# A tile of h in two VectorE instructions with a column each, and one ScalarE pass

## The chip, the cores and the metric

The kernel runs on one core of a Trainium2 chip. The metric is device time in microseconds for one execution; three runs of the kernel before took 1175.74, 1176.55 and 1177.19 us, and their median, 1176.55, is the time to compare with. The engines are named as in the profile: PE is TensorE's matmuls, PEld its weight loads, DVE is VectorE, ACT is ScalarE, POOL is GpSimd, and SP is the queue that starts most transfers.

## What is computed

A decoder trunk of two layers on one sequence of 512 tokens with 1024 channels. Layer 0 mixes tokens with stick-breaking attention, layer 1 with a diagonal state-space layer; each is followed by a gated FFN with a short causal convolution. In front of every mixer and every FFN stands the same small step, and it is the one that the change touches:

```python
def rms_norm(x, g):
    y = xf * lax.rsqrt(jnp.mean(xf * xf, axis=-1, keepdims=True) + EPS)
    return (y * g.astype(jnp.float32)).astype(x.dtype)

def modulate(h, shift, scale):
    return h * (1 + scale[:, None, :]) + shift[:, None, :]
...
    h = modulate(rms_norm(x, norm_mix[i]), sh1, sc1)
```

So h is x times a factor per token (the reciprocal root), times a weight per channel (norm gain times one plus scale), plus a shift per channel. Shift and scale come from a conditioning vector through a matrix-vector product.

## The kernel before

All activations lie transposed: 8 tiles `x[k]` of 128 channels by 512 tokens. Every matrix product is made in three terms for accuracy: each operand is held as a high part (rounded to the matmul's type) and a low part (the value less its high part), and `mm3` (lines 169 to 175) issues high times high, low times high and high times low. In the traces the three have lines 171, 174 and 175. Each weight tile is split in the same way when it arrives (`load_w`, lines 147 to 167): a transfer by SP, the high part on ScalarE (line 165), the low part on VectorE (line 166).

The tiles of h are made by `norm_tile` (lines 302 to 323). For tile k it issues:

- line 308, VectorE: t = x[k] times the factor per token. The factor was broadcast to all partitions by a matmul, so that it is a tile `bc`; in a head it lies in PSUM and is made in two halves of 256 tokens (a full tile then takes two instructions), in attention a copy `rb` in SBUF is used;
- line 315, ScalarE: the high part of t times the weight column `a[:, k]` plus the shift column `b[:, k]`;
- line 317, ScalarE: the same value once more, at full precision, into a tile u;
- line 321, VectorE: the low part, u minus the high part.

The trace names t and u both "nt", the high parts "hH", the low parts "hL", and the weight columns "Amix", "Anorm_ffn" and "Anorm_mix" after the norm that they belong to.

`norm_tile` has two callers.

In attention's V projection (lines 683 to 696) it makes tiles 1 to 7 in full width, one for each turn of a loop; tile 0 is made by hand by other lines (629 to 671), which keep both ScalarE passes. In a turn, ScalarE also makes the high part of the next weight tile (line 568), and the two columns of the next tile (lines 580 and 586) out of row sums that VectorE makes (line 198, a product with accumulation over 1024 columns). VectorE also makes the low part of the weight tile (line 686). Here the instructions are pinned in the order in which the program writes them: `mid` (lines 684 to 688) is placed between the ScalarE passes and the subtraction.

In `head_mm` (lines 326 to 340), which opens the first FFN (near 262 us), the state-space layer (near 634 us) and the second FFN (near 801 us), it makes six tiles in halves, the first half of each and later the second, and then two full tiles: 14 calls. The four output tiles of the head multiply each half as soon as it is there. Within the first halves, at fixed places of TensorE's order, stand the row statistic of the second half (line 266, at tile 1) and the broadcast of its factor (line 288, at tile 3); between them lie a root on ScalarE, five tiny VectorE instructions and the scale matrix `dg` (line 283). The head runs while VectorE still adds the last output tiles of the layer before to the residual (line 355) and sums their squares (lines 244 and 245).

The order of each engine's queue is made at build time by a planner, which simulates the program with a cost for each instruction. What the program pins (`pe_pin`, `keep_in_program_order`) keeps its written order; `follow` and `issue_after` keep an instruction behind another; all the rest goes where the planner's simulation has it ready. The list `pin["head"]` keeps the ScalarE and VectorE instructions of each tile: the weight loads after a head and the preparation of the state-space layer are issued behind them (`behind_head`, lines 342 to 347).

Of the kernel before, what the change touches and what calls it, by code (L numbers as in the profile page):

```python
# [7 lines left out]
F32 = mybir.dt.float32  # L8
# [3 lines left out]
AF = mybir.ActivationFunctionType  # L12
ALU = mybir.AluOpType
# [3 lines left out]
P = 128  # L17
T = 512
# [66 lines left out]
def trunk(tc, I, out, tap=lambda *a: None):  # L85
    with ExitStack() as ctx:
        _trunk(ctx, tc, I, out, tap)


def _trunk(ctx, tc, I, out, tap):  # L90
    nc = tc.nc
    V, S, G, PE, SP = nc.vector, nc.scalar, nc.gpsimd, nc.tensor, nc.sync

    def pool(name, bufs=1, **kw):
        return ctx.enter_context(tc.tile_pool(name=name, bufs=bufs, **kw))
# [5 lines left out]
    np_ = pool("np")  # L101
# [9 lines left out]
    x = [xp.tile([P, T], F32, tag=f"x{k}", name=f"x{k}") for k in range(KD)]  # L111
# [25 lines left out]
    pin = {"head": []}  # L137
# [69 lines left out]
    def mcol(l, v, j):  # L207
        return l * 48 + v * 8 + j
# [90 lines left out]
    def half_cols(ap, cr):  # L299
        return ap.rearrange("p (j c) -> p j c", j=CH)[:, :, cr.start // CH:cr.stop // CH]  # L300

    def norm_tile(h, k, bc, a, b, cr=FULL, pinned=False, first=None, mid=None):
        n = cr.stop - cr.start
        t = np_.tile([P, T], F32, tag="nt1", bufs=2, name="nt1")[:, :n]
        u = np_.tile([P, T], F32, tag="nt2", bufs=1, name="nt2")[:, :n]
        for part in HALF if cr == FULL and isinstance(bc, dict) else (cr,):
            src = bc[part.start] if isinstance(bc, dict) else bc
            pin["nt"] = V.tensor_tensor(t[:, part.start - cr.start:part.stop - cr.start], x[k][:, part], src[:, part], ALU.mult)
        hh, hl = h[0][k][:, cr], h[1][k][:, cr]
        hf = hh.bitcast(F32)  # L310
        keep = pe_pin if pinned else lambda ins: None
        keep(pin["nt"])
        if first:
            first()
        act = S.activation(hh, t, AF.Identity, bias=b[:, k:k + 1], scale=a[:, k:k + 1])
        keep(act)
        aff = S.activation(u, t, AF.Identity, bias=b[:, k:k + 1], scale=a[:, k:k + 1])
        keep(aff)
        if mid:
            mid()  # L320
        dve = V.tensor_tensor(hl, u, hf, ALU.subtract)
        keep(dve)
        pin["head"].append([act, aff, dve])


    def head_mm(R, h, a, b, hd):
        pin["head"] = []
        todo = [(k, HALF[0]) for k in range(HEADK)] + [(k, HALF[1]) for k in range(HEADK)] + [(k, FULL) for k in range(HEADK, KD)]
        made = 0
        for n, (k, cr) in enumerate(todo):  # L330

            while made < (min(n + 3, HEADK) if cr == HALF[0] else n + 1):
                norm_tile(h, todo[made][0], R["bc"], a, b, todo[made][1])
                made += 1
            for q, (w, ps) in enumerate(hd):
                if cr == HALF[0] and (k, q) == HEADS:
                    rstd_stat(R, HALF[1], True)
                if cr == HALF[0] and (k, q) == HEADB:
                    rstd_bc(R, HALF[1], mm, True)
                mm3(ps[:, cr], wk(w, k), (h[0][k][:, cr], h[1][k][:, cr]), k == 0 and cr.start == 0, k == KD - 1)  # L340
# [201 lines left out]
    def attention(acc):  # L542
        with ExitStack() as av_, ExitStack() as ac:
# [139 lines left out]
            for k in range(1, KD):  # L683
                def mid():
                    nxt[0] = high(k + 1) if k < KD - 1 else None
                    pe_pin(V.tensor_tensor(w[1], raws[k], w[0].bitcast(F32), ALU.subtract))
                    if k < KD - 1:
                        gv(1, k + 1)

                nxt = [None]  # L690
                gv(0, k)
                norm_tile(h, k, rb, a, mod[:, 0:KD], FULL, True, None, mid)
                if k + 2 < KD:
                    raws[k + 2] = loads(k + 2)
                prods(k, w)
                w = nxt[0]
# [787 lines left out]
    b = mod[:, mcol(2, 0, 0):mcol(2, 0, 0) + KD]  # L1484
# [154 lines left out]
```

## Time and profile before

The profile shows one execution; the durations in the prediction come from it.

| | |
|---|---|
| median of three runs | 1176.55 us |
| the profiled execution's own time | 1175.82 us |
| its span, first to last instruction | 1174.0 us |
| mean granted TensorE clock | 0.995 |
| data moved | 211.01 MB, 180 GB/s on average |

The span is 1.82 us shorter than the execution's own time. The page gives each engine's busy time and instruction count (the number after the x). A line of a group has the source line, the engine, the operation, output and inputs by name, shapes, the count, then busy time and the mean ns of one, and the idle time of the engine in front of it with what ended it. A line of the timeline has start, duration, engine, source line, operation and names; a bracket shows the idle time in front of it. A matmul's duration there includes the filling of its pipeline, so that matmuls in a row overlap, and the distance from start to start is what one costs. Rows of a table of stretches have start and end, the length, the busy time of PE, PEld, DVE, ACT and POOL with counts, the clock, the share of the DMA engines and GB/s.

### The profile page before, as it was taken

What the parts mean: (1) busy time and instruction counts of PE and PEld (TensorE: products, weight loads), DVE (VectorE), ACT (ScalarE), POOL (GpSimd) and SP (SyncE); (2) the same over time, 40 slices, a digit from 0 to 9 for tenths busy, and PEclk for the clock granted to TensorE, in tenths of its full rate; (3) what the DMA queues carried; (4) which work ended last, traced back from release to release, by engine and by line L of the source; (5) the groups of instructions that cost most, each with busy time, mean ns of one, the idle gap of its engine ahead of it and who ended that gap; (6) DMA issues with size and microseconds to landing.
All of it is one profiled execution on the core that took longest, in us unless ns stands there. A gap on an engine that the chain in (4) does not pass through costs nothing.

```text
span 1174.0 us, 16592 instructions
## 1 busy us (share of the span) xinstructions
PE 1158.9 (99%) x6242; PEld 964.2 (82%) x6242; DVE 857.7 (73%) x1311; ACT 563.5 (48%) x896; POOL 270.8 (23%) x278
## 2 busy tenths in 40 slices
PE   8999999999999999999999999999999999999997
PEld 7887777699788888888889888789888888888887
DVE  6968888775998666787757599887598378744555
ACT  6756667456453244413346477647443144422443
POOL 2001110000298799979800000000000000000003
PEclk8999999999999999999999999999999999999999
DMA  8873656331267858797756598671176357432322
GB/s 320 292 264 116 192 162 195 111 123 55 78 189 268 247 167 252 198 292 253 230 151 223 149 353 293 207 255 50 49 231 217 107 153 184 133 123 73 92 69 72
DMA packets 91618, 211.01 MB, mean 180 GB/s; under 512 B 19601, under 2 KB 37905, under 8 KB 91538
## 3 DMA queue, kind: packets, MB, share of 16 engines
q1 hardware_dynamic: 78562, 191.08, 51.0%
q0 software_dynamic: 4656, 16.78, 4.5%
q10 hardware_dynamic: 8320, 2.10, 0.8%
q8 instruction: 49, 0.80, 0.3%
q14 instruction: 31, 0.25, 0.1%
HBM read 188.68 MB, written 21.24 MB: 179 GB/s over the span
## 4 chain that ended last, share of the span: by engine, by line
PE 78%; DVE 7%; issue 7%; DMA 5%; ACT 2%; POOL 1%; SPq 1%; POOLq 0%; DVEq 0%; ACTq 0%
PE up L171 13%; PE up L174 13%; PE up L175 13%; PE dn L171 6%; PE dn L174 6%; PE dn L175 6%; DMA wg<-in_w_modT_dram 3%; PE u L174 1%; PE u L171 1%; PE u L175 1%; PE wo L171 1%; PE wos L174 1%; PE wo L175 1%; PE wo L174 1%; PE wos L175 1%
## 5 line engine op out<-in xcount | busy, mean ns | idle before, releaser
L171 PE MATMUL up<-hH,up_h 128*128 128x512 f32 x640 | 249.7, 391 | 0.3 <-DVE ca L461 0.3
L175 PE MATMUL up<-hH,up_l 128*128 128x512 f32 x640 | 249.3, 390 | 0.3 <-DVE up_l L166 0.3
L174 PE MATMUL up<-hL,up_h 128*128 128x512 f32 x640 | 249.3, 390 | 0.0
L461 DVE SCALAR_TENSOR_TENSOR ca<-up,small,ca 128x511 f32<-128x511 f32 (+1 forms) x176 | 131.6, 748 | 120.7 <-ACT ca L459 117.6
L171 PE MATMUL dn<-gH,dn_h 128*128 128x512 f32 (+1 forms) x394 | 145.0, 369 | 0.0
L198 DVE SCALAR_TENSOR_TENSOR wg<-wg,cact 128x1024 f32<-128x1024 f32 x96 | 121.4, 1281 | 31.7 <-DMA wg<-in_w_modT_dram 31.6
L174 PE MATMUL dn<-gL,dn_h 128*128 128x512 f32 (+1 forms) x394 | 144.5, 367 | 0.0
L175 PE MATMUL dn<-gH,dn_l 128*128 128x512 f32 (+1 forms) x394 | 144.4, 366 | 0.0
L171 PEld LDWEIGHTS up<-hH,up_h 128*128 128x128 f32 x640 | 120.1, 188 | 26.5 <-issue 1.5
L175 PEld LDWEIGHTS up<-hH,up_l 128*128 128x128 f32 x640 | 120.1, 188 | 25.9 <-DVE up_l L166 1.1
L174 PEld LDWEIGHTS up<-hL,up_h 128*128 128x128 f32 x640 | 120.1, 188 | 24.4
L459 ACT ACTIVATE ca<-up,small 128x512 f32<-128x512 f32 x88 | 68.2, 775 | 149.5 <-PE up L175 149.5
L1511 POOL TENSOR_SCALAR xa<-x,Anorm_out 128x256 f32<-128x256 f32 x7 | 5.7, 818 | 570.3 <-DVE x L355 570.3
L165 ACT ACTIVATE up_h<-up_r 128x1024 fp32r<-128x1024 f32 x80 | 84.2, 1052 | 75.3 <-PE dn L174 58.1
L166 DVE TENSOR_TENSOR up_l<-up_r,up_h 128x1024 fp32r<-128x1024 f32 x80 | 116.3, 1454 | 5.4 <-ACT up_h L165 4.5
L355 DVE SCALAR_TENSOR_TENSOR x<-dn,mod,x 128x512 f32<-128x512 f32 (+1 forms) x55 | 37.4, 680 | 71.4 <-PE dn L175 71.4
L171 PEld LDWEIGHTS dn<-gH,dn_h 128*128 128x128 f32 x394 | 74.3, 189 | 12.9 <-issue 0.6
L174 PEld LDWEIGHTS dn<-gL,dn_h 128*128 128x128 f32 x394 | 74.3, 189 | 12.1
L175 PEld LDWEIGHTS dn<-gH,dn_l 128*128 128x128 f32 x394 | 74.3, 189 | 12.1
L165 ACT ACTIVATE dn_h<-dn_r 128x1024 fp32r<-128x1024 f32 (+1 forms) x48 | 46.7, 982 | 46.2 <-PE dn L174 38.5
L166 DVE TENSOR_TENSOR dn_l<-dn_r,dn_h 128x1024 fp32r<-128x1024 f32 (+1 forms) x48 | 61.6, 1283 | 0.8 <-ACT dn_h L165 0.5
L477 ACT ACTIVATE gH<-gm 128x512 fp32r<-128x512 f32 x44 | 27.1, 616 | 67.3 <-DVE gm L473 67.3
(349 smaller groups left out, 2311.0 us busy)
## 6 DMA issues: line engine op xcount, KB each, us to landing
up_r<-in_w_up_dram SPq DMA_DIRECT2D x80, 512.0 KB
wg<-in_w_modT_dram SPq DMA_DIRECT2D x71, 512.0 KB
dn_r<-in_w_down_dram SPq DMA_DIRECT2D x32, 512.0 KB
wg<-in_w_modT_dram POOLq DMA_DIRECT2D x25, 512.0 KB, 4.0
wgs<-in_w_modT_dram SPq DMA_DIRECT2D x16, 512.0 KB
dn_r<-in_w_down_dram SPq DMA_DIRECT2D x16, 384.0 KB
wv_r<-in_w_v_dram SPq DMA_DIRECT2D x8, 512.0 KB
wk_r<-in_w_qk_dram SPq DMA_DIRECT2D x8, 512.0 KB
```

Source lines behind the costliest of these rows:

```text
L165: order("S", lambda: S.activation(wh[:, :n], raw[:, :n], AF.Copy))
L166: pin["split"] = order("V", lambda: V.tensor_tensor(wl[:, :n], raw[:, :n], wh[:, :n].bitcast(F32), ALU.subtract))
L171: ins = PE.matmul(ps, ah, bh, start=start, stop=False)
L174: PE.matmul(ps, ah, bl, start=False, stop=False)
L175: PE.matmul(ps, al, bh, start=False, stop=stop)
L198: mul = lambda: V.scalar_tensor_tensor(w, w, 1.0, cact, ALU.mult, ALU.mult, accum_out=raw[:, col:col + 1])
L355: add = lambda: V.scalar_tensor_tensor(xs, pv, gate, xs, ALU.mult, ALU.add)
L459: follow("S", lambda: S.activation(ca, ps, AF.Identity, bias=small[:, cb:cb + 1], scale=tapw[2]))
L461: follow("V", lambda: V.scalar_tensor_tensor(ca[:, q:], ps[:, :T - q], tapw[2 - q], ca[:, q:], ALU.mult, ALU.add))
L477: follow("S", lambda: S.activation(gh, m, AF.Copy))
L1511: G.tensor_scalar(xa[k], x[k][:, cb], a[:, k:k + 1], 0.0, ALU.mult, ALU.add)
```

## The change

The product on line 308 takes the weight column along: (x times a) times the factor, one three-operand VectorE instruction. ScalarE then only adds the shift and rounds to the high part. The second ScalarE pass and its tile u are gone; the subtraction becomes (t plus shift) minus the high part, again one three-operand VectorE instruction. `pin["head"]` keeps two instructions for each tile in place of three. Tile 0 of attention, which has its own lines, isn't changed, and no transfer is.

```diff
     def norm_tile(h, k, bc, a, b, cr=FULL, pinned=False, first=None, mid=None):
         n = cr.stop - cr.start
         t = np_.tile([P, T], F32, tag="nt1", bufs=2, name="nt1")[:, :n]
-        u = np_.tile([P, T], F32, tag="nt2", bufs=1, name="nt2")[:, :n]
         for part in HALF if cr == FULL and isinstance(bc, dict) else (cr,):
             src = bc[part.start] if isinstance(bc, dict) else bc
-            pin["nt"] = V.tensor_tensor(t[:, part.start - cr.start:part.stop - cr.start], x[k][:, part], src[:, part], ALU.mult)
+            pin["nt"] = V.scalar_tensor_tensor(t[:, part.start - cr.start:part.stop - cr.start], x[k][:, part], a[:, k:k + 1], src[:, part], ALU.mult, ALU.mult)
         hh, hl = h[0][k][:, cr], h[1][k][:, cr]
-        hf = hh.bitcast(F32)
...
-        act = S.activation(hh, t, AF.Identity, bias=b[:, k:k + 1], scale=a[:, k:k + 1])
+        act = S.activation(hh, t, AF.Identity, bias=b[:, k:k + 1])
         keep(act)
-        aff = S.activation(u, t, AF.Identity, bias=b[:, k:k + 1], scale=a[:, k:k + 1])
-        keep(aff)
         if mid:
             mid()
-        dve = V.tensor_tensor(hl, u, hf, ALU.subtract)
+        dve = V.scalar_tensor_tensor(hl, t, b[:, k:k + 1], hh.bitcast(F32), ALU.add, ALU.subtract)
         keep(dve)
-        pin["head"].append([act, aff, dve])
+        pin["head"].append([act, dve])
```

## Prediction

> **What bounds the kernel now.** I read the page first, then the busy time in the four stretches where the changed helper runs, then who waits for whom, and last the timeline around each wait.
>
> ```profile
> span 1174.0 us, 16592 instructions
> ...
> PE 1158.9 (99%) x6242; PEld 964.2 (82%) x6242; DVE 857.7 (73%) x1311; ACT 563.5 (48%) x896; POOL 270.8 (23%) x278
> ```
> ```profile
> 22.00:66.00 44.00, 44.00 (x195) 36.27 (x195) 40.99 (x60) 32.28 (x56) 0.00 (x0) 1.00 0.85 276
> ...
> 255.00:300.00 45.00, 45.00 (x298) 41.09 (x297) 28.41 (x81) 25.75 (x43) 0.18 (x2) 1.00 0.16 48
> ...
> 632.00:660.00 28.00, 27.75 (x201) 26.06 (x200) 20.37 (x53) 21.78 (x39) 0.00 (x0) 1.00 0.50 175
> ...
> 800.00:835.00 35.00, 35.00 (x231) 31.83 (x230) 20.90 (x46) 23.20 (x38) 0.00 (x0) 1.00 0.18 61
> ```
>
> TensorE is busy for 1158.9 of 1174.0 us. The columns of the second answer are the stretch, its length, then PE, PEld, DVE, ACT and POOL busy, the clock, and DMA. The first stretch is the V projection of attention, which calls the helper for tiles 1 to 7. The other three are the heads of the first FFN, of the state-space layer and of the second FFN, where the helper makes h from the residual. In the first, second and fourth TensorE is never without a matmul. In the third it lacks 0.25 us. So ScalarE's load there (half to four fifths of the time) is not what ends these stretches. It can matter only where TensorE stands for a tile of h. The next answers show who stands for the operation that goes.
>
> ```profile
>   DVE hL L321: 10.7, 21
> ```
> ```profile
> PE u L174 <- DVE hL L321: 0.2, 1, 0.2
> ```
> ```profile
> PEld up L174 <- DVE hL L321: 0.6, 2, 0.3
> ```
>
> The first line is from the view of line 317, the second ScalarE pass, under those who waited for it: VectorE's low-part subtraction stood 10.7 us in 21 places. The other two are from TensorE's and the weight loads' lists of waits: of those 10.7 us only one matmul and two weight loads pass anything on. All the other idle time of VectorE is hidden behind matmuls already queued.
>
> **The change, part by part.** The helper runs 49 times: three heads with 12 half tiles (256 columns) and 2 full tiles (512), and seven full tiles in V. These are the prices of what it issues, and of the nearest operations of the forms that it will issue.
>
> ```profile
> L317 ACT ACTIVATE nt<-nt,mod,Anorm_ffn 128x256 f32<-128x256 f32 x24 | 14.3, 596 | 0.3 <-DVE hL L321 0.3
> L315 ACT ACTIVATE hH<-nt,mod,Anorm_ffn 128x256 fp32r<-128x256 f32 x24 | 14.2, 590 | 4.5 <-DVE nt L308 4.5
> ...
> L315 ACT ACTIVATE hH<-nt,mod,Amix 128x512 fp32r<-128x512 f32 x7 | 5.7, 817 | 2.2 <-DVE nt L308 2.1
> ```
> ```profile
> L459 ACT ACTIVATE ca<-up,small 128x512 f32<-128x512 f32 x88 | 68.2, 775 | 149.5 <-PE up L175 149.5
> ...
> L813 ACT ACTIVATE wT<-t,ones 128x512 f32<-128x512 f32 x16 | 10.3, 684 | 24.5 <-PE t L810 24.5
> ```
> ```profile
> L461 DVE SCALAR_TENSOR_TENSOR ca<-up,small,ca 128x511 f32<-128x511 f32 x88 | 65.8, 747 | 117.9 <-ACT ca L459 117.6
> ...
> L308 DVE TENSOR_TENSOR nt<-x,rbc 128x256 f32<-128x256 f32 x48 | 18.9, 415 | 2.1 <-PE rbc L288 2.0
> ...
> L321 DVE TENSOR_TENSOR hL<-nt,hH 128x256 fp32r<-128x256 f32 x36 | 15.3, 424 | 7.8 <-ACT nt L317 7.6
> ...
> L355 DVE SCALAR_TENSOR_TENSOR x<-wos,mod,x 128x512 f32<-128x512 f32 x5 | 6.0, 1206 | 0.0
> ...
> L1322 DVE TENSOR_TENSOR m<-pv,pR 128x512 f32<-128x512 f32 x8 | 5.5, 690 | 9.7 <-PE pv L1280 9.6
> ...
> L308 DVE TENSOR_TENSOR nt<-x,rb 128x512 f32<-128x512 f32 x7 | 4.8, 683 | 0.0
> ```
>
> Removed: 49 ScalarE passes, 36 of 256 columns at 0.596 us (21.5 us) and 13 of 512 at about the 0.817 of their twin on line 315 (10.6 us), together 32 us of ScalarE's 563.5. On the path of one tile that is one ScalarE pass less between the first product and the low part.
>
> Changed on ScalarE: the high part loses its scale column and keeps its bias column. Line 459 has both columns and takes 775 ns, line 813 has the bias column alone and takes 684 ns, both from PSUM, so I take 0.09 us off each of the 49; the bounds are no gain and 0.13 us (817 less 684, which mixes sources).
>
> Changed on VectorE: 55 products (48 of half tiles, 7 of full ones) and 49 subtractions become three-operand instructions with a column. Line 461 is that form: 747 ns against 683 for the plain product, so 0.064 us more each, 104 x 0.064 = 6.7 us of VectorE in all. The bounds are no cost and the dearest such row, line 355 on wos, whose operands are strided: 1206 less 683, 0.52 us each. I take 0.064, since line 461 has contiguous operands, as the new ones do. Lines 1322 and 308 have one PSUM source and none, and cost 690 and 683, so the 64 ns are the column's rather than PSUM's.
>
> [...]
>
> What hides the 6.7 us. In a head a half tile feeds 12 matmuls of about 0.12 us (half the slot of a 512-column one, below), 1.4 us, and VectorE's two operations for it are 0.415 + 0.424 + 2 x 0.064 = 0.97 us; VectorE was idle for 27 to 40% of the head stretches, and of its 10.7 us of standing most go. In V the cover is thinner, and shown below.
>
> What TensorE gets back. These rows show the three places where it stood for hL.
>
> ```profile
> 634.65 0.73 PE L171 MATMUL u<-hH,win_h 128*128 128x256 f32 x4
> 635.63 0.38 PE L174 MATMUL u<-hL,win_h 128*128 128x256 f32 x1 [0.24 <-DVE hL L321]
> ```
> ```profile
> 634.76 0.48 DVE L355 SCALAR_TENSOR_TENSOR x<-dn,mod,x 128x256 f32<-128x256 f32 x1 [0.46 <-PE dn L175]
> 635.16 0.41 DVE L321 TENSOR_TENSOR hL<-nt,hH 128x256 fp32r<-128x256 f32 x1
> ```
> ```profile
> 634.51 0.59 ACT L317 ACTIVATE nt<-nt,mod,Anorm_mix 128x256 f32<-128x256 f32 x1
> ```
> ```profile
> 272.49 0.39 PE L171 MATMUL up<-hH,up_h 128*128 128x512 f32 x1
> 272.87 0.39 PE L174 MATMUL up<-hL,upo_h 128*128 128x256 f32 x1
> ```
> ```profile
> 811.43 0.39 PE L171 MATMUL up<-hH,up_h 128*128 128x512 f32 x1
> 811.79 0.39 PE L174 MATMUL up<-hL,uph_h 128*128 128x256 f32 x1
> ```
>
> State-space head: four 256-column matmuls start at 634.65. Their 0.73 us covers a filled pipeline, and they leave it free for the next from about 635.13 to 635.39; the next starts at 635.63, so 0.24 to 0.50 us are lost. Line 317 ended at 635.10 and the subtraction came at 635.16, but behind a residual update on VectorE (634.76, 0.48) that waits for TensorE. With line 317 gone the subtraction is ready about when that pass used to start, 634.51, ahead of that update, if the planner puts it there; then all of the loss goes. If it stays behind, nothing goes, and the longer form adds 0.06. I take 0.4 saved, bounds -0.5 and +0.06.
>
> FFN heads: a 512-column matmul takes one slot of about 0.23 us (V's 24 per tile in 5.44 us, below). The next follow after 0.38 and 0.36 us, so 0.15 and 0.13 are lost. The subtraction now ends about 0.5 us sooner, so both go: 0.28 saved, bounds -0.28 and 0. What is late next is the last matmul in front, that is TensorE itself.
>
> The added wait. The product now reads the scale column, which ScalarE alone read before. In the heads that column is a vector written long before (first and second FFN):
>
> ```profile
> L229 DVE SCALAR_TENSOR_TENSOR Anorm_ffn<-mod,small x2: 159/161/163, 197.3 to 791.0; 128x8 f32<-128x8 f32 x2
> ```
>
> The heads' first products come at 260 and 799 us. In V it is made column by column by ScalarE, and behind a product that waits for it stand, on VectorE's queue, the weight split of the same tile, the next column's row sum, and the low part.
>
> ```profile
> 29.89 0.68 DVE L308 TENSOR_TENSOR nt<-x,rb 128x512 f32<-128x512 f32 x1
> ...
> 34.52 0.68 DVE L308 TENSOR_TENSOR nt<-x,rb 128x512 f32<-128x512 f32 x1
> ...
> 53.05 0.69 DVE L308 TENSOR_TENSOR nt<-x,rb 128x512 f32<-128x512 f32 x1
> ```
> ```profile
> 43.36 1.98 PE L171 MATMUL v<-wv_h,hH 128*128 128x512 f32 x8
> ...
> 48.80 1.98 PE L171 MATMUL v<-wv_h,hH 128*128 128x512 f32 x8
> ```
> ```profile
> 52.37 0.39 ACT L586 ACTIVATE Amix<-mod,small 128x1 f32<-128x1 f32 x1
> ```
>
> VectorE's turn is 34.52 - 29.89 = 4.63 us and has no gap; TensorE's is 48.80 - 43.36 = 5.44 us. With two dearer operations VectorE's becomes 4.63 + 0.13 = 4.76, still shorter. At the upper bound it would be 4.63 + 1.05 = 5.68, and TensorE would lose 0.24 us in each of six turns, 1.4 us. The column for the last tile is written by 52.76 and wanted at 53.05: a margin of 0.29 us, and VectorE can lose 0.68 us in a turn before TensorE notices. So V is worth 0, bounds 0 and +1.4.
>
> Nothing is moved past a DMA queue: the helper issues no transfer, and the weight loads that follow a tile keep the high and low parts as their marks.
>
> The sum: -0.4 - 0.28 + 0 = about -0.7 us, bounds -0.8 and +1.5. The profiled execution took 1175.82 us (span 1174.0 and 1.82 around it) and would take 1175.1; the median of the three runs, 1176.55, lies 0.73 above it, so I predict 1175.85 us. A measurement of this kernel can tell about 0.2%, 2.35 us, from no change, and 0.7 is 0.06%.
>
> **The rivals.** First, every chain start is paid back: each head has two half-tile chains, and if TensorE's queue were refilled a whole ScalarE pass sooner in all six, 6 x 0.596 = 3.6 us would go, 1173.0 us. For it: the passes are in series with the first low part. Against it: only three of the six have a wait at all, and TensorE's whole shortage there is known.
>
> Second, VectorE's standing is what sets the pace, and its 10.7 us come off: 1165.9 us. Against it stand the stretches with TensorE never idle. [...]
>
> Third, slower: the second half's statistic comes late. In a head the scale matrix dg of the second half passes through VectorE's queue, and its broadcast on TensorE stands at a fixed place in the order, with the rest of the head behind it.
>
> ```profile
> 267.98 0.48 DVE L283 TENSOR_SCALAR dg<-consts,ny 128x128 f32<-128x128 f32 x2
> 268.38 1.22 DVE L166 TENSOR_TENSOR up_l<-up_r,up_h 128x1024 fp32r<-128x1024 f32 x1
> ```
> ```profile
> 270.17 0.59 PE L288 MATMUL rbc<-dg,ones 128*128 128x256 f32 x2
> ```
>
> dg ends at 268.46 and the broadcast starts at 270.17: 1.7 us of cover. The weight split behind it (1.22 us) waits for a ScalarE pass, and with ScalarE lighter it can be ready before dg. A plan that puts this split and two tiles' pairs (2 x 0.97) ahead of dg delays it 3.16 us, 1.45 past the cover, 4.4 us in three heads: 1180.9 us. It decides from a delay of 1.7 us in a head, and is over 2.35 us in sum from 2.5. For it: these instructions are left to the planner. Against it: the tiles themselves finish sooner, so one split alone (1.22) fits the cover, and the pairs have mostly gone by then.
>
> That the change doesn't do what it says can't be: two instructions of each tile become one form and a third is not issued.
>
> **How the numbers follow.** Forecast, small gain or none with V's bound inside: 0.80. All chain starts: 0.06. VectorE's standing: 0.02. Late statistic, or another order of the planner that costs over 2.35 us: 0.12, since the order is made anew for the whole program, and TensorE's idle time to be won by one is only 1174.0 - 1158.9 = 15 us in all, while what can be lost has no such end. Faster by over 0.2% is 0.06 + 0.02 = 0.08, same 0.80, slower 0.12. The range goes down to 1174.2, which is past the lower bound (1175.75) less the spread of the runs (lowest 1175.74, 0.81 below the median) and ends where faster begins. It goes up to 1178.7, the upper bound of +1.5 and the spread on that side (1177.19, 0.64 above). What it leaves out is the 0.08 and the 0.12, 0.2 in all.
>
> **What would show it.** Right: line 317's group gone; the high part at about 0.50 us (256) and 0.72 (512); product and subtraction near 0.48 and 0.75; the waits of TensorE for hL gone or under 0.1; VectorE's turn in V near 4.76 us, without a gap ahead of the product, and TensorE's unchanged at 5.44; the head stretches shorter by some tenths. Wrong: TensorE idle in front of the second broadcast, a VectorE gap that ends with the scale column in V, or a difference of more than 2.35 us in a stretch where the helper doesn't run, which would be the planner's.

## The result and the profile after

The changed kernel takes 1182.80 us (median of four runs, 1181.24 to 1184.79) against 1176.14 for the kernel before (four runs, 1175.49 to 1177.19): a ratio of 1.0057, 95% interval 1.0037 to 1.0076, slower by 6.7 us. Run once more (e7 below, six runs) it took 1184.24 against 1176.14, ratio 1.0067 (1.0051 to 1.0082). The prediction, 1175.85 within 1174.2 to 1178.7, was wrong, on the wrong side.

In the changed kernel line 315 is line 314, line 321 is line 318, and whatever lies behind the helper is three lines higher up (most of the later runs have the old numbers there). First the page, then groups of instructions, with shapes kept apart.

```profile
span 1182.1 us, 16546 instructions
...
PE 1160.6 (98%) x6242; PEld 964.2 (82%) x6242; DVE 861.4 (73%) x1311; ACT 533.1 (45%) x847; POOL 275.0 (23%) x278
```
```profile
L314 ACT ACTIVATE hH<-nt,mod 128x256 fp32r<-128x256 f32 x36 | 17.1, 503 | 27.7 <-DVE nt L308 26.6 <-PE wo L175 1.0
L318 DVE SCALAR_TENSOR_TENSOR hL<-nt,mod,hH 128x256 fp32r<-128x256 f32 x36 | 16.3, 478 | 1.1 <-ACT hH L314 1.1
...
L318 DVE SCALAR_TENSOR_TENSOR hL<-nt,mod,hH 128x512 fp32r<-128x512 f32 x13 | 9.4, 746 | 0.0
L314 ACT ACTIVATE hH<-nt,mod 128x512 fp32r<-128x512 f32 x13 | 9.4, 722 | 2.6 <-DVE nt L308 2.5
...
L308 DVE SCALAR_TENSOR_TENSOR nt<-x,Amix,rb 128x512 f32<-128x512 f32 x7 | 5.2, 746 | 0.4 <-ACT Amix L583 0.4
```

The instructions cost what was forecast: 0.48 and 0.75 us on VectorE, 0.50 and 0.72 on ScalarE, and ScalarE is lighter by 30 us. VectorE's low part stands for ScalarE for 1.1 us, where it stood for 10.7. Yet the span of the profiled execution grew by 8.1 us. The next two views say where: the busy time in the three heads, over the same stretches as in the prediction, and the list of what TensorE waited for.

```profile
255.00:300.00 45.00, 43.88 (x305) 40.73 (x305) 28.65 (x75) 17.03 (x30) 0.18 (x2) 1.00 0.19 58
632.00:660.00 28.00, 26.50 (x210) 25.38 (x209) 22.06 (x57) 11.71 (x23) 0.00 (x0) 1.00 0.40 152
800.00:835.00 35.00, 33.89 (x251) 31.95 (x250) 22.93 (x56) 11.83 (x23) 0.00 (x0) 1.00 0.16 48
```
```profile
PE up L171 <- ACT hH L314: 2.2, 2, 1.1
...
PE t L807 <- DVE om L795: 1.9, 5, 0.6
PE wo L174 <- DVE oL L927: 1.6, 1, 1.6
PE pz L1351 <- ACT yn L1346: 1.6, 3, 0.6
PE pk L1137 <- POOL cl L1200: 1.2, 1, 1.2
PE u L171 <- ACT hH L314: 1.1, 1, 1.1
```

TensorE was never idle in the two FFN heads and lacked 0.25 us in the other. Now it lacks 1.12, 1.50 and 1.11 us. In each head it stands once, for 1.1 us, for a high part. Two more names come back below: pk is a product in the preparation of the state-space layer, which falls into the first FFN's stretch and reads a table cl made by GpSimd; pz is a transpose in that layer, which reads a copy yn made by ScalarE. So the kernel got slower just where the prediction said that nothing could be late.

One head in detail. The first fence is TensorE's timeline of the kernel before, the second the same place after; both begin with the statistic of the second half.

```profile
265.94 0.50 PE L266 MATMUL stat<-ones,acc 128*128 128x1 f32 x4
...
270.42 0.82 PE L171 MATMUL up<-hH,upo_h 128*128 128x256 f32 x4
271.07 0.28 PE L174 MATMUL up<-hL,upo_h 128*128 128x256 f32 x1
...
272.02 0.63 PE L171 MATMUL up<-hH,upo_h 128*128 128x256 f32 x4
```
```profile
271.01 0.50 PE L266 MATMUL stat<-ones,acc 128*128 128x1 f32 x4
...
274.81 0.28 PE L175 MATMUL up<-hH,upo_l 128*128 128x256 f32 x1
274.93 0.59 PE L288 MATMUL rbc<-dg,ones 128*128 128x256 f32 x2
276.64 0.74 PE L171 MATMUL up<-hH,upo_h 128*128 128x256 f32 x4 [1.11 <-ACT hH L314]
```

Before, the broadcast (270.17) was followed by the 12 matmuls of the last first-half tile, from 270.42 to 272.02, and under them the first tile of the second half was made. After, nothing of the first half is left behind the broadcast, so TensorE stands from the end of the broadcast until that tile comes. VectorE isn't the one that is late:

```profile
267.84 0.42 DVE L245 TENSOR_TENSOR acc<-acc,sq 128x256 f32<-128x256 f32 x1
...
272.69 0.49 DVE L283 TENSOR_SCALAR dg<-consts,ny 128x128 f32<-128x128 f32 x2
```

The sum of squares is complete at 268.26, and the statistic comes 2.75 us later. dg ends at 273.18, 1.75 us ahead of the broadcast, about the cover of 1.7 us that it had before. It is TensorE's own order that holds both back. I had called their places fixed, and they are not: a pinned instruction is only kept behind the one in front of it in the program, and the matmuls of later tiles, which aren't pinned, may pass. In the built programs, compared with each other, the second half's statistic stands 15, 4 and 15 matmuls later in the three heads, its broadcast 12, 20 and 12. There are 21 pieces in a different order in TensorE's queue, 22 in VectorE's, 11 in ScalarE's and 5 in SP's, in V, the heads and around the state-space layer.

### The profile page after: what moved, and what is told of

The parts are those of the page before. It is cut to its first block, busy times and chain, and to the rows that moved or that the text cites. A ratio compares the mean times of both kernels' runs of the same rounds, so it can differ in the third digit from the quotient of the medians.

```text
span 1182.1 us, 16546 instructions
## 1 busy us (share of the span) xinstructions
PE 1160.6 (98%) x6242; PEld 964.2 (82%) x6242; DVE 861.4 (73%) x1311; ACT 533.1 (45%) x847; POOL 275.0 (23%) x278
## 4 chain that ended last, share of the span: by engine, by line
PE 68%; POOL 8%; DMA 8%; DVE 8%; issue 3%; ACT 2%; SPq 0%; POOLq 0%; ACTq 0%; DVEq 0%
PE up L171 11%; PE up L174 11%; PE up L175 11%; PE dn L171 6%; PE dn L175 5%; PE dn L174 5%; DMA wg<-in_w_modT_dram 2%; PE o L823 1%; PE wo L171 1%; PE wos L174 1%; PE wo L175 1%; PE wo L174 1%; PE wos L175 1%; PE wos L171 1%; PE t L807 1%
## 5 line engine op out<-in xcount | busy, mean ns | idle before, releaser
L458 DVE SCALAR_TENSOR_TENSOR ca<-up,small,ca 128x511 f32<-128x511 f32 (+1 forms) x176 | 131.5, 747 | 119.1 <-ACT ca L456 116.0
```

The lines of the kernel that those rows point to most:

```text
L458: follow("V", lambda: V.scalar_tensor_tensor(ca[:, q:], ps[:, :T - q], tapw[2 - q], ca[:, q:], ALU.mult, ALU.add))
```

## The experiments

My theory was now that the planner's new order makes the loss; the rival, that the 104 dearer VectorE instructions do. To tell them apart I tied each instruction behind the one that is to stand in front of it on its engine, so that a kernel can be run in another's order:

```diff
     with tile.TileContext(nc, schedule_with_timeline_sim=True) as tc:
         trunk(tc, aps, out)
+        for eng, order in places.items():
+            for p, q in zip(order, order[1:]):
+                tc.add_manual_dep(made[eng][q], made[eng][p].name, behind, reason="place")
```

`made` holds an engine's instructions as the program writes them, `places` the wanted order, `behind` an edge that fixes the order and waits for nothing.

In the table attention runs from the start of the first V matmul to the start of the statistic behind the output projection; the first FFN from there to the first statistic of the state-space head; that layer to the first statistic of the second FFN's head; and the last stretch to the end of the last matmul. The profile of each run gives these times, so they are of one execution, while the medians are of all. A ratio is against the kernel before as it ran beside that run, and so isn't the quotient of two medians of the table. For the changed kernel the marks are:

```profile
21.71 0.71 PE L649 MATMUL v<-wv_h,hH 128*128 128x512 f32 x2
...
259.25 0.50 PE L266 MATMUL stat<-ones,acc 128*128 128x1 f32 x4
...
633.53 0.58 PE L266 MATMUL stat<-ones,acc 128*128 128x1 f32 x4
...
801.74 0.61 PE L266 MATMUL stat<-ones,acc 128*128 128x1 f32 x4
...
1174.70 0.85 PE L1515 MATMUL fin<-consts,xa 128*128 128x128 f32 x6
```

| run | instructions; order | attention | FFN 1 | state space | FFN 2 | median us | ratio to before (95%) |
|---|---|---|---|---|---|---|---|
| before, first profile | old; old | 234.61 | 373.34 | 165.61 | 372.60 | 1176.14 | |
| after | new; new | 237.54 | 374.28 | 168.21 | 373.81 | 1182.80 | 1.0057 (1.0037 to 1.0076) |
| e1 | new; old | 237.56 | 372.81 | 164.66 | 372.33 | 1177.29 | 1.0008 (0.9998 to 1.0018) |
| e2 | old; new | 236.17 | 375.14 | 173.50 | 374.17 | 1188.02 | 1.0100 (1.0084 to 1.0116) |
| e3 | new; new, old in attention | 237.51 | 374.84 | 166.48 | 373.79 | 1181.96 | 1.0040 (1.0024 to 1.0056) |
| e4 | new; new, old in the heads | 235.16 | 372.94 | 165.31 | 372.44 | 1179.18 | 1.0040 (1.0023 to 1.0056) |
| e5 | new; new, TensorE's old in the heads | 236.73 | 372.76 | 166.40 | 372.34 | 1180.31 | 1.0029 (1.0015 to 1.0044) |
| e6 | old; old, TensorE's new in the heads | 236.72 | 375.08 | 166.80 | 375.16 | 1183.66 | 1.0063 (1.0051 to 1.0075) |
| e7 | after, again | 238.41 | 374.35 | 168.72 | 373.68 | 1184.24 | 1.0067 (1.0051 to 1.0082) |
| e8 | before, again (one run) | 235.45 | 373.59 | 164.30 | 372.59 | 1175.53 | |
| e9 | old, V dearer by 2.7 us; old | 237.52 | 373.60 | 166.24 | 372.70 | 1178.91 | 1.0021 (1.0007 to 1.0035) |
| e10 | new in the heads alone; old | 233.83 | 373.39 | 164.64 | 372.35 | 1174.87 | 0.9988 (0.9973 to 1.0002) |
| e11 | new in V alone; old | 237.43 | 373.02 | 164.45 | 372.60 | 1177.06 | 1.0006 (0.9992 to 1.0020) |
| e12 | e10, weight parts on GpSimd | 239.43 | 372.93 | 166.07 | 372.33 | 1179.55 | 1.0033 (1.0019 to 1.0048) |
| e13 | new; new, places held | 238.50 | 372.18 | 167.41 | 372.29 | 1178.37 | 1.0019 (1.0005 to 1.0032) |
| e14 | new in the heads alone; new, places held | 235.08 | 376.65 | 166.51 | 372.29 | 1181.58 | 1.0034 (1.0006 to 1.0061) |

**Order against instructions: e1 and e2.** All queues are exchanged.

> The changed kernel's instructions, each engine's queue held in the order that the planner gave the kernel before (each instruction is tied behind the one in front of it; of the order only the second ScalarE pass is missing). If the 6.7 us come from the planner's new order, this runs like the kernel before or less: 1175 to 1177 us, and with the prediction's sum of -0.7 us near 1175.5. If they come from the dearer VectorE instructions (104 of them at +0.064 us, 6.7 us in all) or from the wait on the weight column, it keeps them: 1181 to 1184 us.

> The instructions of the kernel before, in the order that the planner gave the changed kernel, the second ScalarE pass put right behind the first. If the order is the cause, it is as slow as the changed kernel, 1181 to 1185 us (a little more, if the second pass delays the first tiles of a half). If the VectorE instructions are the cause, 1175 to 1178 us.

e1 took 1177.29 us, 1.0008: no measurable difference from before, with all the dearer instructions in it. e2 took 1188.02, slower than the changed kernel, with none of them. The order is the cause, though these two runs don't yet say which part of it. In that order the new instructions even help, by 4 to 5 us (1188.02 against 1182.80 and 1184.24); most of it lies in the state-space layer (173.50 us in e2, 168.21 after).

**Which part of the order: e3 and e4.** Only the differing pieces of a region are put back.

> The changed kernel in its own order, save that in attention (V projection and the weight splits and loads behind it) the queues stand in the order of the kernel before. By the theory of the order, with attention 2.9 us late in the trace: about 1180 us (1179 to 1181), the heads still slow. By the theory of the VectorE instructions: 1182 to 1183, unchanged.

> The changed kernel in its own order, save that in the three heads the queues of TensorE, VectorE and ScalarE stand in the order of the kernel before. By the theory of the order the waits of about 1.1 us for the first tile of the second half go, in all three heads: 1179 to 1180 us, attention still slow by 2.9. By the theory of the VectorE instructions: 1182 to 1183, unchanged.

The medians are 1181.96, 1 us above what the theory gave, and 1179.18, within it; the ratios are the same, 1.0040, so the whole times can't tell the two regions apart. The profile of e3 says something else than I expected: attention took 237.51 us with its old order too. By this one profile, what it loses isn't its order's. e4's profile, of its fastest execution (1174.77 us), is without the heads' waits: behind attention it is 5.6 us shorter than after's (910.69 against 916.30).

**TensorE's queue alone: e5 and e6.** Of the three heads' order, only TensorE's is put back (e5), or only TensorE's is spoiled in the kernel before (e6).

> The changed kernel in its own order, save TensorE's queue in the three heads, which stands as in the kernel before: the second half's statistic 15, 4 and 15 matmuls sooner and its broadcast 12, 20 and 12 sooner. VectorE's and ScalarE's queues are the new ones. If TensorE's order alone makes the waits of 1.1 us in each head, it comes out like the run with all three queues restored, 1178.5 to 1180.5 us. If VectorE's order (the last sum of squares 0.7 us later) makes them, the statistic stands in front of TensorE by about that much and the time stays at 1181.5 to 1183.

> The kernel before in its own order, save TensorE's queue in the three heads, which stands as in the changed kernel: statistic and broadcast of the second half later. All instructions are the old ones. If the later place is a cause by itself, TensorE waits about 1.1 us or more for the first tile of the second half in each head, and the time is 1178 to 1180 us; if it costs only together with the dearer VectorE instructions, 1176 to 1177.

e6 settles it. Pieces of 249 instructions of TensorE in another order, with none of them changed, cost 7.5 us (1183.66, 1.0063). All the pieces of the three heads are exchanged in it, not the statistic and the broadcast alone. The list of TensorE's waits has the same high parts in it, and low parts as well, since the old chain of a tile is longer (before its low part stand two ScalarE passes of 0.59 and 0.60 us for a half tile in the kernel before, one of 0.50 in the changed one):

```profile
PE up L171 <- ACT hH L315: 2.3, 2, 1.1
...
PE up L174 <- DVE hL L321: 1.4, 4, 0.5
PE u L171 <- ACT hH L315: 1.1, 1, 1.1
```

e5 shows the reverse, 1180.31 us. Its heads have TensorE busy throughout, as before, but for 0.58 us in the second:

```profile
255.00:300.00 45.00, 45.00 (x303) 41.49 (x302) 29.58 (x81) 17.25 (x30) 0.18 (x2) 1.00 0.14 48
632.00:660.00 28.00, 27.42 (x201) 25.73 (x200) 22.09 (x55) 11.95 (x23) 0.00 (x0) 1.00 0.51 186
800.00:835.00 35.00, 35.00 (x236) 32.20 (x235) 22.21 (x48) 14.97 (x25) 0.00 (x0) 1.00 0.17 49
```

The sums of the last three stretches give the price. New instructions: 916.30 and 916.75 in TensorE's new order (after, e7), 909.80, 910.69 and 911.50 in its old one (e1, e4, e5), so 5.9 us. Old instructions: 917.04 (e6) against 911.55 and 910.48 (before, e8), so 6.0. And at the same old order of TensorE the new instructions are worth 910.66 less 911.02, -0.4 us. In all these stretches the granted clock was 1.00.

**How much is the execution's: e7 and e8.**

> The changed kernel as it is, once more beside the others: 1181 to 1184 us. Its profile shows whether the 2.9 us that attention lost in the first profile stay (then they belong to the kernel) or move (then they belong to the execution). In the runs so far attention lost between 0.5 and 2.9 us with either set of instructions and either order, so I expect between 0 and 3, not the same again.

> The kernel before as it is, once more: 1175 to 1178 us. If attention's time is the execution's, the stretch from the first V matmul to the first statistic behind the output projection, 234.6 us in the first profile, is longer here by some tenths to 2 us; if it belongs to the kernel, it is 234.6 again.

Both happened: attention was 0.87 us longer in the second profile of the changed kernel and 0.84 in the second of the one before. One profile of attention says little. With the old forms in V (before, e2, e6, e8, e10, e14) its mean is 235.31 us, over 233.83 to 236.72; with the new ones (after, e1, e3, e4, e5, e7, e11, e13) 237.36, over 235.16 to 238.50. The difference is 2.0 us with an interval of 0.8 to 3.3. Part of the scatter is TensorE's clock: in e6 it was 0.51 for about 3.4 us from 205.8, which cost 1.7 of attention's 236.72 us (an estimate: half of that stretch), and without that the difference is 2.3 (1.2 to 3.4). Among the profiles with the new forms the order makes no difference (237.50 us in the old one, 237.27 in the planner's). The old forms stand in the planner's new order of attention in one profile only, e2, at 236.17, so that a share of the order isn't excluded there. TensorE's wait for the masked scan of attention (om, on VectorE) says the same: 1.9 to 3.1 us in all eight profiles with the new forms, 0.2 to 0.7 with the old ones, but for e2 with 1.9.

**V by itself: e9, e10, e11.** All three stand in the old order. e9 makes the low part of four tiles twice:

```diff
         dve = V.tensor_tensor(hl, u, hf, ALU.subtract)
         keep(dve)
+        if pinned and k <= 4:
+            pe_pin(V.tensor_tensor(hl, u, hf, ALU.subtract))
```

e10 and e11 choose the helper's form by its caller (`new = not pinned`, and `new = pinned`).

> The kernel before, its order kept, with one VectorE operation too many in V: the low part of tiles 1 to 4 is made twice, at 0.68 us each, 2.7 us in all, three times the 0.9 us that the new forms add in V. VectorE's turn becomes 5.31 us, still under TensorE's 5.44, so by the prediction's reading (V worth 0 while VectorE's turn is the shorter) nothing changes: 1175.5 to 1177.5. If VectorE's lateness is handed on to the work behind V (weight splits, v's eviction, the row sums) and from there to TensorE, the time rises by about 1.5 to 3 us: 1177.7 to 1179.5.

> The change made in the three heads alone (42 of the 49 tiles), V as before, and all queues in the order of the kernel before. The prediction's sum for the heads, -0.7 us, gives 1175.5 to 1176; the traces of the runs with the old order in the heads showed -0.3 behind attention. No measurable difference is expected, 1174.8 to 1177.2. If the new VectorE forms cost time in the heads, over 1178.

> The change made in V alone (7 of the 49 tiles), the heads as before, all queues in the order of the kernel before. If V is worth 0, 1175.5 to 1177. If the 0.06 us that each new VectorE form adds pile up in V (0.9 us by its end) and reach TensorE, with attention some 1.4 us longer as the profiles so far suggest (2.5 us over the first profile in the mean of six with the new forms, 1.1 in four with the old): 1177 to 1178.5.

e9 took 1178.91, 1.0021: of the 2.7 us added, 2.5 (0.8 to 4.1) reached the end, though VectorE's turn stayed under TensorE's. V's VectorE time isn't hidden. The profile of one execution shows part of the way: TensorE stood for om for 1.9 us until 114.63, and behind that its clock was low once more (0.56 from 116.0 to 119.6), about 1.6 of attention's 237.52 us. e11 shows how 0.06 us piles up. These are its products for tiles 1 and 7 and the first row sum behind V, and then that row sum in the kernel before.

```profile
25.20 0.74 DVE L309 SCALAR_TENSOR_TENSOR nt<-x,Amix,rb 128x512 f32<-128x512 f32 x1
...
53.71 0.75 DVE L309 SCALAR_TENSOR_TENSOR nt<-x,Amix,rb 128x512 f32<-128x512 f32 x1
...
93.55 1.22 DVE L198 SCALAR_TENSOR_TENSOR wg<-wg,cact 128x1024 f32<-128x1024 f32 x1
```
```profile
25.25 0.69 DVE L308 TENSOR_TENSOR nt<-x,rb 128x512 f32<-128x512 f32 x1
...
93.01 1.23 DVE L198 SCALAR_TENSOR_TENSOR wg<-wg,cact 128x1024 f32<-128x1024 f32 x1
```

VectorE's turn is (53.71 - 25.20) / 6 = 4.75 us, 4.76 having been forecast. From tile 1 to tile 7 that makes 28.51 us against 27.80 before (25.25 to 53.05), 0.71 later, and at the row sum it is 0.59 (68.35 against 67.76 us behind the product of tile 1). The waits of TensorE between 60 and 262 us, for e11 and then for e10, whose V is the old one:

```profile
PE t L810 <- DVE om L798: 2.0, 4, 0.9
PE wo L174 <- DVE oL L930: 1.4, 1, 1.4
```
```profile
PE t L810 <- DVE om L798: 0.7, 2, 0.5
```

So the rest of attention hands on VectorE's lateness, by the masked scan (om) and the low part of the heads' output (oL). The sign rests on e9 and on the profiles of attention; the size stays open: by the medians e11 costs +0.7 us (-0.9 to +2.4), by the profiles of attention 2.0. e10 took 1174.87, -1.4 us (-3.2 to +0.2): the shortest median of all, and not measurably faster than before.

**An attempt at a faster kernel: e12.** If V's VectorE time counts, relieving it should pay.

```diff
-                    pe_pin(V.tensor_tensor(w[1], raws[k], w[0].bitcast(F32), ALU.subtract))
+                    pe_pin((G if k in (2, 4, 6) else V).tensor_tensor(w[1], raws[k], w[0].bitcast(F32), ALU.subtract))
```

> The run with the change in the heads alone and all queues in the order of the kernel before, and in V the low part of three weight tiles (2, 4 and 6) made by GpSimd, which is idle there, in place of VectorE: VectorE is relieved of 3 x 1.14 = 3.4 us in V. If VectorE's lateness behind V is what the work after it pays for, the opposite of the run with the dearer V follows: attention shorter by up to 2 us, 1172.5 to 1174.5, faster than both kernels. If V's VectorE queue is hidden, or if GpSimd's work slows VectorE as much as it relieves it, 1174.5 to 1176.5 like the run without it.

It took 1179.55, 1.0033 to e10's 0.9988. The first of the moved operations, and what VectorE did meanwhile:

```profile
29.46 2.49 POOL L686 TENSOR_TENSOR wv_l<-wv_r,wv_h 128x1024 fp32r<-128x1024 f32 x1 [9.12 <-ACT wv_h L568]
```
```profile
27.86 1.22 DVE L198 SCALAR_TENSOR_TENSOR wgs<-wgs,cact 128x1024 f32<-128x1024 f32 x1
...
29.61 3.42 DVE L198 SCALAR_TENSOR_TENSOR wgs<-wgs,cact 128x1024 f32<-128x1024 f32 x1
```

The row sum that met GpSimd's operation took 3.42 us in place of 1.22. GpSimd ended at 31.95, the row sum 1.08 later. What held it the profile doesn't show. So VectorE was later and not earlier: its product for the last tile came 32.77 us behind that for tile 1, against 27.80 in e10. As a relief this told nothing. As a bigger dose it goes the way of e9, but attention's 239.43 us hold two things that aren't VectorE's lateness behind V: a wait of 1.1 us for a high part in V itself, and 1.7 us of low clock behind a wait of 1.85 for om.

**Holding the places in the program: e13 and e14.** No order is borrowed here. Tiles 3 and 4 stay behind the statistic, tile 5 behind the broadcast:

```diff
                 if cr == HALF[0] and (k, q) == HEADS:
                     rstd_stat(R, HALF[1], True)
+                    held[3] = held[4] = R["hold"]
                 if cr == HALF[0] and (k, q) == HEADB:
                     rstd_bc(R, HALF[1], mm, True)
+                    held[5] = R["hold"]
-                mm3(ps[:, cr], ...)
+                with tc.issue_after(held[k].ins) if cr == HALF[0] and k in held else ExitStack():
+                    mm3(ps[:, cr], ...)
```

> The changed kernel in the planner's own order, with one rule added in the heads: the first-half matmuls of tiles 3 and 4 stay behind the second half's statistic, those of tile 5 behind its broadcast. The broadcast then stands where it stood in the kernel before (in the state-space head 8 matmuls later), the statistic 8, 4 and 8 matmuls later. If the late place is the cause, the three waits of 1.1 us go and the time is like that of the run with TensorE's old order in the heads, 1179 to 1181 us, V's share left in it. If something else in the new order makes them, 1182 to 1184.

> The same rule with the change in the three heads alone, V as before, in the planner's own order, nothing taken from the kernel before. If the late place costs some 5 us and V's forms the rest, this is level with the kernel before or a little under it: 1175 to 1178 us. If the rest of the planner's new order costs time too, 1178 to 1181.

e13 took 1178.37, and its heads have no wait for a high part any more. Behind attention it takes 911.88 us (916.30 and 916.75 without the rule), so the rule gives back 4.6 of the 5.9: the three waits, 3.3, and that for cl, 1.2, are gone. What e13 has left, 1.0019 or 2.2 us, is about V's share. e14 was a miss, 1181.58, with a wide interval. In its profile TensorE stands 3.0 us for the table cl (1.2 us in after), and then runs at about half its clock:

```profile
432.84 0.43 PE L1145 MATMUL pk<-cl,bd 128*32 128x128 f32 x8 [3.02 <-POOL cl L1208]
...
434.40 0.63 PE L171 MATMUL up<-hH,up_h 128*128 128x512 f32 x1
434.82 0.63 PE L174 MATMUL up<-hL,up_h 128*128 128x512 f32 x1
...
437.41 0.39 PE L175 MATMUL up<-hH,up_l 128*128 128x512 f32 x1
437.64 0.40 PE L171 MATMUL up<-hH,up_h 128*128 128x512 f32 x1
```

From start to start a matmul takes 0.43 us and later 0.23, and the granted clock from 433.5 to 437.0 was 0.51. The wait and 1.7 us of low clock are what the first FFN's stretch, 376.65 us, has over e13's 372.18. The twelve runs of e14 go with the clock too: 1172.84 us at 0.999, 1186.82 to 1190.50 at 0.990 to 0.992. The wait for cl is in after, e2, e3, e7 and e14, and not in e4, e5 and e13, which have the planner's own order of the rest too; what makes it stays open.

## Why the prediction was wrong

**The step that failed** is the reason given against the third rival, that "the tiles themselves finish sooner" and so the statistic's cover holds. With it the sum put a new order of TensorE's queue at nothing. What the runs showed in its place: the planner put more of the first half's matmuls ahead of the statistic and the broadcast, used up the work that hid the second half's chain (broadcast, product, high part: 1.7 us from 274.93 to 276.64), and so laid it bare. The new order of the heads costs 5.9 us behind attention with the new instructions and 6.0 with the old ones (e6). The order is the planner's alone, so it can be read from a built program without a run: with the change in V alone the heads' order stays; with the change in the heads alone it is the changed kernel's; with the new VectorE forms but the second ScalarE pass kept as a plain copy the broadcast already moves by 12 matmuls, the statistic doesn't. In that last program the pass still stands ahead of the low part, so tiles that are ready sooner can't be the whole reason. Why the planner's simulation prefers the new order stays open.

**The third rival** had the place right, the second half's statistic and broadcast, and the wrong mechanism: dg wasn't late on VectorE, its cover stayed at 1.75 us. It was priced 4.4 us; the new order of the heads turned out at 5.9, so the price was near by luck. Of the 5.9 the three waits for high parts are 3.3 and pk's 1.2; in after, pz's wait for yn grew by 1.2 (0.4 to 1.6), but hardly in e3 (0.5). With the old instructions (e6) pk doesn't wait, and waits for low parts come in its stead. The chance of 0.12, which took in any other order of the planner, was too low, since nothing more was needed.

**V worth 0** failed as well, by a smaller size. VectorE's turn was right to 0.01 us; the comparison with TensorE's turn was the wrong one. VectorE in V doesn't wait for TensorE. It runs ahead of it, in e11 without a gap between the products for tiles 1 and 7 (25.20 to 53.71), so each 0.06 us makes it later (0.71 there) with all that it does behind V (0.59 at the first row sum). The bound of +1.4 came from another mechanism and is near the measured 0.7 to 2.0 by luck.

**The added wait** did show once, in the planner's new order: the last product waits 0.40 us for its column, where a margin of 0.29 had been found.

```profile
54.62 0.75 DVE L308 SCALAR_TENSOR_TENSOR nt<-x,Amix,rb 128x512 f32<-128x512 f32 x1 [0.40 <-ACT Amix L583]
```

**The gain in the heads**, -0.7 us, came out at -0.4 in profiles (same TensorE order), too small to be told from none: two profiles of the kernel before differ by 1.1 in those stretches (911.55 and 910.48). The state-space head's wait for hL didn't go: it is 0.33 us (0.24 before), close to the bound on the side of a loss, since the subtraction stayed behind the residual update. **The prices** of the new forms were right to 10 ns. That VectorE's extra in the heads, 90 of the 104 operations or 5.8 of the 6.7 us, is hidden was right too (e10).

## What to carry to other kernels

Where a planner orders the queues, a change of instructions is two changes. Compare the built orders before you price anything, and run the new instructions in the old order: that told more than any other run here. Where a chain must start early (a statistic, a broadcast), hold the filling work behind it explicitly, since being pinned behind its neighbour doesn't keep others from passing. And where an engine has no gap in a stretch, don't take it for hidden because another engine's turn is longer (in e9 2.5 of the 2.7 us added to the shorter turn reached the end): ask what it does next.

## What the runs showed of the hardware

In e12 a VectorE row sum of 128x1024 that started 0.15 to 0.16 us into a GpSimd subtraction of that size (2.49 to 2.50 us) took 3.41 to 3.42 us in place of 1.22, in each of three tiles, and ended 1.07 to 1.08 us behind it (the mean of all 14 row sums there was 1689 ns, against 1214 in e10).

The three-operand form with a 128x1 column cost VectorE 58 to 63 ns more than the two-operand one at 512 elements (746 against 688 and 683) and 54 to 60 at 256 (478 against 424, 475 against 415), whether one of the other operands lies in PSUM or all in SBUF.

Behind four waits of TensorE, of 1.85 (e6, e12), 1.90 (e9) and 3.02 us (e14), came a stretch of about 3.4 us in which matmuls took nearly twice as long (in e14 0.43 us from start to start in place of 0.23), which cost about 1.6 to 1.7 us each time (an estimate from the granted clock, 0.51 to 0.58 in these stretches). Three other waits of 1.86 to 1.97 us (e2, e13, e7) had none behind them, and no shorter one had, in these profiles between 24 and 1160 us.

Attention's time moved by 0.9 us between two profiles of one program, and by 3.3 between two kernels whose queues are the same up to the first head (235.16 us in e4, 238.41 in e7), so a share of it needs several profiles.
